# Hybrid encoder layer in fp32r, 1 core: warm-up matmuls on a constant, the second input piece cast in two parts, the second raw input in one transfer

## The chip, the core and the metric

The kernel runs on one core of a Trainium2 chip. The metric is the device time of one execution in microseconds (us). Names of engines: PE is TensorE's matmul, PEld its weight load, DVE is VectorE, ACT is ScalarE, POOL is GpSimd, SP is SyncE, which here only issues transfers (DMA). Times of the timeline count from the start of the profiled span.

## The reference

One layer on a sequence of 1024 frames with 1024 features, all in float32:

```
h = x @ w_in + b_in                     # 1024 x 6144, split in xa za xb zb ga gb
ya = rg_lru(causal_conv4(xa)) * silu(za)          # a scan over the frames
yb = multiscale_pool(xb) * silu(zb)               # windows 2, 4, 8, 16
y  = (sigmoid(ga) * (ya @ w_proj_a) + sigmoid(gb) * (yb @ w_proj_b)) @ w_out + b_out
out = layer_norm(2**0.25 * x + y) * ln_gain + ln_bias
```

The five large products are x @ w_in (1024 x 1024 x 6144), the two projections and w_out (each 1024 x 1024 x 1024), and the pooling product of four 256 x 256 blocks.

## The kernel before, in words

**Products.** Every float32 operand is split into two fp32r parts: `hi` is a cast on ScalarE, `lo` is the raw value minus `hi`, on VectorE (`split`, L450). A product then is three matmuls: hi x hi, hi x lo, lo x hi (`passes`, L454). In a row of the profile `ps_s<-x13l,w0h` is such a matmul: output tile, moving operand, stationary operand. The large products use a seven-product scheme on 2 x 2 blocks, so that sums of input quarters are operands too: `t13` (`t` in the rows) is such a sum of raw input (`sum57`, L1042).

**Order of the work.** Nothing is emitted directly. Each instruction is recorded as a task (`Plan`, L162; the line that emits all of them later is L388, which therefore stands in nearly every row of the profile). `Plan.order` (L252) then plays the tasks through with an estimated duration for each (`cost`, L214) and a due time that is counted back from the matmul that needs the result. TensorE and GpSimd keep the order in which the program recorded their work; ScalarE, VectorE and SyncE take, of what is ready, the task that is due first. So a change of a few tasks can change the order of others on these three engines, wherever due times or free buffers shift.

**Transfers.** Transfers of SP and ACT share eight completion semaphores in turn. The ninth transfer is issued only when the first has landed, and so on.

**The start.** The input arrives transposed in four pieces q of 128 x 2048, each as two raw tiles of 128 x 1024: `xr[q][0]` and `xr[q][1]`. Their halves of 512 columns are four quarters (kh, h) of the piece (`raws`): the first half of `xr[q][0]` is (0,0), its second half is (1,1), the first half of `xr[q][1]` is (0,1), called `xb`, and the second is (1,0), called `x`. Quarters (0,0) and (1,1) are the tiles `x13h` and `x13l`. The first product takes two blocks of weights, `w0r` raw, `w0h` and `w0l` split, and runs quarter by quarter as data comes in (`mm0`), each quarter with both blocks, in four output banks `ps_s`. For piece 0 the quarter (0,0) is loaded, cast, subtracted and multiplied in two parts of 256 columns (`PARTS`), all other quarters in one of 512.

Before it, six matmuls of 128 x 512 zeros run into a bank that nobody reads (`WARM`, L954 to L958). Their operand `warm` is the first half of a work tile of the pool `kt`, which VectorE sets to zero.

**The rest.** 22 groups for the branches a, g (gates) and b follow to about 496 us, then the projections and the output product to 731 us, and a last layer norm with its stores to 738.3 us. The change has no code there.

Of the kernel before, what the change touches and what calls it, by code (L numbers as in the profile page):

```python
# [11 lines left out]
F32 = mybir.dt.float32  # L12
F32R = mybir.dt.float32r
AF = mybir.ActivationFunctionType
ALU = mybir.AluOpType

P = 128
# [3 lines left out]
H = 512  # L21
# [2 lines left out]
EPS = 1e-5  # L24
WINDOWS = (2, 4, 8, 16)
PAD = 16
WARM = 6
NW = 10
NR = 4
NWORK = 10  # L30
# [370 lines left out]
def layer_kernel(ctx: ExitStack, tc: tile.TileContext, xq, x, w_in, par, wg, w_pool, wpa, wpb, w_out, rows, out):  # L401
# [16 lines left out]
    def xt(name, dt=F32R, shape=(P, 2, H)):  # L418
        return xpool.tile(list(shape), dt, tag="x", name=name)
# [7 lines left out]
    def kt(name, dt=F32):  # L427
        return kpool.tile([P, S], dt, tag="k", name=name)
# [4 lines left out]
    def bank(name):  # L433
        return psum.tile([P, H], F32, tag="ps", name=name)
# [5 lines left out]
    HALF = [slice(0, H), slice(H, S)]  # L440
    V, A = nc.vector, nc.scalar
# [508 lines left out]


    begin = ctx.enter_context(ExitStack())
    pass
    warm = kt("warm", F32R)[:, :H]  # L954
    V.memset(warm.bitcast(F32), 0.0)
    psw = bank("ps_warm")
    for i in range(WARM):
        nc.tensor.matmul(psw, warm[:, 0:P], warm, start=True, stop=True)  # L958
# [4 lines left out]
    xr = [[kt(f"xr{q}_{i}", F32) for i in range(2)] for q in range(KQ)]  # L963
# [7 lines left out]
    def dma_w0(n, a, b, h=slice(0, 2)):  # L971

        (A if a == 0 else nc.sync).dma_start(w0_part(wr, n, a, b)[:, h], w_in[first[n]].rearrange("p (h k) m -> p h k m", h=2)[:, h, a:b, :])

    def split_w0(n, a, b, h=slice(0, 2)):
        split(*(w0_part(t, n, a, b)[:, h] for t in (wr, wh, wl)))

    def dma_x(q, i, sl=slice(0, S)):
        nc.sync.dma_start(xr[q][i][:, sl], xq[q, i][:, sl])
# [10 lines left out]
    def split_x(q, kh, h, sl=slice(0, H)):  # L990
        i, p = raws[kh, h]
        split(xr[q][i][:, HALF[p]][:, sl], *(t[:, sl] for t in quarter(q, kh, h)))
# [3 lines left out]
    def mm0(q, kh, h, n, cs=slice(0, H)):  # L996
        sl = slice(q * P, (q + 1) * P)
        passes(ps0[n][h][:, cs], (wh[n][:, kh, sl], wl[n][:, kh, sl]), tuple(t[:, cs] for t in quarter(q, kh, h)),
               q == 0 and kh == h and cs.start == 0, q == KQ - 1 and kh != h)


    PARTS = [slice(0, H // 2), slice(H // 2, H)]
# [4 lines left out]
    dma_w0(0, 0, 1, slice(1, 2))  # L1007
    dma_w0(1, 0, 1)
    dma_x(0, 0, HALF[1])
    dma_x(0, 1, HALF[0])  # L1010
    dma_x(0, 1, HALF[1])
    dma_w0(0, 1, 2)
    dma_x(1, 0)
    dma_w0(1, 1, 2)
# [10 lines left out]
    t13, t24 = [None] * KQ, [None] * KQ  # L1025
# [15 lines left out]

    def sum57(q):  # L1042
        t13[q] = xt(f"t13_{q}", F32)
        r = xr[q][0].rearrange("p (i s) -> p i s", i=2)
        V.tensor_tensor(t13[q], r, xr[q][1][:, HALF[0]].unsqueeze(1).to_broadcast((P, 2, H)), ALU.subtract)

# [35 lines left out]
    for kh, h in ((0, 0), (1, 1), (0, 1), (1, 0)):  # L1082
        if kh == h == 1:
            split_w0(0, 0, 1, slice(1, 2))
        for sl in PARTS if kh == h == 0 else (slice(0, H),):
            split_x(0, kh, h, sl)
            mm0(0, kh, h, 0, sl)
        if kh == h == 1:
            split_w0(1, 0, 1)
            mm0(0, 0, 0, 1)  # L1090
        if kh or h:
            mm0(0, kh, h, 1)
# [6 lines left out]
    w = weights_steps(1)  # L1099
    lower, upper = (0, 1), (2, 3)  # L1100
    each(sum57, lower)
    parts(2)
    each(hi57, lower)
    each(lo57, lower)
    parts(3)
    hi(w.ra, w.pair("wa", (1, 2))[0])
    each(sum57, upper)
    lo(w.ra, *w.tiles["wa"])
    w.sums75(wt("sb_A0", F32))
# [247 lines left out]
    for i, (n, j) in enumerate(steps):  # L1357
# [10 lines left out]
        for g in range(KQ):  # L1368
# [5 lines left out]
            for q in range(KQ):  # L1374
                sl = slice(q * P, (q + 1) * P)
# [10 lines left out]
            if (n, j) in DONE:  # L1386
                d, h = DONE[n, j]
# [198 lines left out]
```

## Time and profile before

| | |
|---|---|
| times of three runs | 740.8, 741.32, 739.7 us; median 740.8 |
| the profiled execution | 740.07 us, of which the span is 738.3 |
| granted TensorE clock, mean | 0.998 |
| busy: PE / DVE / ACT / POOL | 99% / 81% / 62% / 9% of the span |
| bytes moved by DMA | 158.98 MB, mean 215 GB/s |

The profile is that of one execution. The time of an execution is a little longer than its span, here by 1.8 us, which lies around the first and last instruction. A row of the timeline has the start, the time the instructions of the row took, the engine, the operation, output and inputs with their shapes, how many instructions stand in the row, and in brackets for how long the engine had been idle and on whom it waited. Matmuls overlap: the time of one is longer than the distance to the next.

### The profile page before, as it was taken

What the parts mean: (1) busy time and instruction counts of PE and PEld (TensorE: products, weight loads), DVE (VectorE), ACT (ScalarE), POOL (GpSimd) and SP (SyncE); (2) the same over time, 40 slices, a digit from 0 to 9 for tenths busy, and PEclk for the clock granted to TensorE, in tenths of its full rate; (3) what the DMA queues carried; (4) which work ended last, traced back from release to release, by engine and by line L of the source; (5) the groups of instructions that cost most, each with busy time, mean ns of one, the idle gap of its engine ahead of it and who ended that gap; (6) DMA issues with size and microseconds to landing.
All of it is one profiled execution on the core that took longest, in us unless ns stands there. A gap on an engine that the chain in (4) does not pass through costs nothing.

```text
span 738.3 us, 8785 instructions
## 1 busy us (share of the span) xinstructions
PE 729.5 (99%) x3249; PEld 599.4 (81%) x3249; DVE 600.8 (81%) x741; ACT 459.0 (62%) x587; POOL 67.9 (9%) x119
## 2 busy tenths in 40 slices
PE   9999999999999999999999999999999999999996
PEld 7887888888787878788888888888888888888885
DVE  7999796969696878977986768879948786999686
ACT  7686959686877868688844445447553545315473
POOL 0171011111101111100011100100000000000021
PEclk9999999999999999999999999999999999999999
DMA  9247979588988989842187954999679996758748
GB/s 320 111 142 198 264 180 279 135 240 224 303 161 217 328 206 282 219 113 91 54 204 154 212 114 158 278 315 331 235 241 303 311 333 234 267 201 232 196 80 149
DMA packets 64227, 158.98 MB, mean 215 GB/s; under 512 B 4340, under 2 KB 8308, under 8 KB 64120
## 3 DMA queue, kind: packets, MB, share of 16 engines
q1 hardware_dynamic: 43512, 106.26, 41.4%
q0 software_dynamic: 20112, 51.91, 33.6%
q8 instruction: 25, 0.41, 0.2%
q10 hardware_dynamic: 560, 0.26, 0.1%
q14 instruction: 18, 0.15, 0.1%
HBM read 137.43 MB, written 77.07 MB: 291 GB/s over the span
## 4 chain that ended last, share of the span: by engine, by line
PE 99%; DVE 1%; DVEq 0%; issue 0%
PE a_A L388 11%; PE a_B L388 11%; PE a_G L388 11%; PE oa L388 6%; PE pa_a L388 6%; PE pa_b L388 6%; PE c_B L388 6%; PE c_A L388 6%; PE c_G L388 5%; PE ps_s L388 3%; PE oc L388 3%; PE pc_b L388 3%; PE pc_a L388 3%; PE ps_pool L388 3%; PE e_B L388 3%; PE e_A L388 3%
## 5 line engine op out<-in xcount | busy, mean ns | idle before, releaser
L388 ACT ACT_TABLE_LOAD x38 | 48.8, 1283 | 3.0 <-issue 2.3
L388 DVE TENSOR_TENSOR i<-i,xc 128x1024 f32<-128x1024 f32 x8 | 9.8, 1225 | 26.9 <-ACT i L388 26.9
L388 DVE SCALAR_TENSOR_TENSOR xc<-xp,par_sb,xc 128x1023 f32<-128x1023 f32 (+2 forms) x24 | 30.7, 1281 | 0.5
L388 PE MATMUL pa_a<-oh,oh 128*128 128x512 f32 x64 | 24.9, 389 | 0.0
L388 PE MATMUL pa_a<-ol,oh 128*128 128x512 f32 x64 | 24.9, 389 | 0.0
L388 PE MATMUL pa_a<-oh,ol 128*128 128x512 f32 x64 | 24.9, 389 | 0.0
L388 PE MATMUL pa_b<-oh,oh 128*128 128x512 f32 x64 | 24.9, 389 | 0.0
L388 PE MATMUL pa_b<-ol,oh 128*128 128x512 f32 x64 | 24.9, 389 | 0.0
L388 PE MATMUL pa_b<-oh,ol 128*128 128x512 f32 x64 | 24.9, 389 | 0.0
L388 ACT ACTIVATE zb<-zb,par_sb 128x1024 f32<-128x1024 f32 (+1 forms) x16 | 15.0, 938 | 14.2 <-DVE zb L388 14.1
L388 ACT ACTIVATE r<-ps_g,par_sb 64x512 f32<-64x512 f32 x32 | 21.9, 683 | 2.1 <-DVE rb_B L388 0.8
L388 ACT ACTIVATE i<-ps_g,par_sb 64x512 f32<-64x512 f32 x32 | 21.9, 684 | 1.9 <-DVE r L388 1.4
L388 PE MATMUL c_A<-x64h,wd_A 128*128 128x512 f32 x64 | 21.0, 389 | 0.0
L388 PE MATMUL c_B<-x64h,wd_B 128*128 128x512 f32 x64 | 21.0, 389 | 0.0
L388 POOL DMA_DIRECT2D out<-y x7 | 8.5, 1210 | 130.0 <-ACT sd L388 117.4
L388 PE MATMUL ps_pool<-mixh,wp 128*128 128x512 f32 x64 | 20.3, 389 | 0.0
L388 PE MATMUL e_A<-x,wah_A 128*128 128x512 f32 x64 | 19.7, 389 | 0.0
L388 PE MATMUL e_B<-x,wah_B 128*128 128x512 f32 x64 | 19.7, 389 | 0.0
L388 POOL COPY paced<-pace 128x1 f32<-128x1 f32 x17 | 6.4, 376 | 130.9 <-ACT pace L388 130.9
L388 PE MATMUL c_G<-x64h,wd_G 128*128 128x512 f32 x56 | 18.4, 389 | 0.0
L388 DVE TENSOR_TENSOR_SCAN r<-a,i 128x1024 f32<-128x1024 f32 x8 | 18.3, 2284 | 0.1
L388 PE MATMUL e_G<-x,wah_G 128*128 128x512 f32 x56 | 17.2, 389 | 0.0
(521 smaller groups left out, 2534.5 us busy)
## 6 DMA issues: line engine op xcount, KB each, us to landing
sg<-sg SPq DMA_DIRECT2D x16, 512.0 KB, 4.3
ra_A<-in_w_in SPq DMA_DIRECT2D x8, 512.0 KB, 7.1
rb_A<-in_w_in SPq DMA_DIRECT2D x8, 512.0 KB, 7.5
xb<-bias SPq DMA_DIRECT2D x4, 1024.0 KB, 12.8
ya<-r SPq DMA_DIRECT2D x8, 512.0 KB, 5.7
xb<-in_x POOLq DMA_DIRECT2D x4, 1024.0 KB, 8.8
ra_B<-in_w_in SPq DMA_DIRECT2D x8, 512.0 KB, 4.3
rb_B<-in_w_in SPq DMA_DIRECT2D x8, 512.0 KB, 6.6
```

The costliest lines, as they stand in the source:

```text
L388: getattr(getattr(nc, t.op[0]), t.op[1])(*a, **k)
```

## The change

It has four parts.

1. The warm-up matmuls read the constant zero of 128 x 1 that the program's own preamble sets, repeated along the free dimension, in place of the work tile; VectorE's memset falls away, and so does the work tile. There are eight instead of six.
2. The quarter (1,1) of piece 0 is cast, subtracted and multiplied in two parts of 256 columns, like (0,0). (`kh else` is true for kh = 1; for (0,0) the parts were there already, by the same expression: `PARTS if kh == h else`.)
3. The sum `t13` of piece 0 is done by two instructions of 512 columns instead of one of 1024.
4. `xr[0][1]` comes in one transfer of 128 x 1024 instead of two of 128 x 512.

```diff
-WARM = 6
+WARM = 8
...
-    warm = kt("warm", F32R)[:, :H]
-    V.memset(warm.bitcast(F32), 0.0)
+    warm = tc.nc.const_aps.tensor(0.0, [P, H]).bitcast(F32R)
     psw = bank("ps_warm")
     for i in range(WARM):
         nc.tensor.matmul(psw, warm[:, 0:P], warm, start=True, stop=True)
...
     dma_x(0, 0, HALF[1])
-    dma_x(0, 1, HALF[0])
-    dma_x(0, 1, HALF[1])
+    dma_x(0, 1)
     dma_w0(0, 1, 2)
     dma_x(1, 0)
...
     def sum57(q):
         t13[q] = xt(f"t13_{q}", F32)
+        if q == 0:
+            for i in range(2):
+                V.tensor_tensor(t13[q][:, i, :], xr[q][0][:, HALF[i]], xr[q][1][:, HALF[0]], ALU.subtract)
+            return
...
     for kh, h in ((0, 0), (1, 1), (0, 1), (1, 0)):
         if kh == h == 1:
             split_w0(0, 0, 1, slice(1, 2))
-        for sl in PARTS if kh == h == 0 else (slice(0, H),):
+        for sl in PARTS if kh == h else (slice(0, H),):
             split_x(0, kh, h, sl)
             mm0(0, kh, h, 0, sl)
```

The rows below are the order of instructions on an engine, before and after; a number behind a name is that of the buffer, which the change shifts.

TensorE at the start, before. `ps_s_0` and `ps_s_1` are the output banks; the first six real matmuls are the quarter (0,0), then comes (1,1):

```order
L388 MATMUL ps_warm<-warm 128x512 x6
L388 MATMUL ps_s_0_150<-x13h_142,w0h_145 128x256
L388 MATMUL ps_s_0_150<-x13l_147,w0h_145 128x256
L388 MATMUL ps_s_0_150<-x13h_142,w0l_152 128x256
...
L388 MATMUL ps_s_1_168<-x13h_142,w0h_145 128x512
L388 MATMUL ps_s_1_168<-x13l_147,w0h_145 128x512
L388 MATMUL ps_s_1_168<-x13h_142,w0l_152 128x512
L388 MATMUL ps_s_0_178<-x13h_142,w0h_165 128x512
```

and with the change:

```order
L388 MATMUL ps_warm<-const-float32-0.0 128x512 x8
L388 MATMUL ps_s_0_149<-x13h_141,w0h_144 128x256
...
L388 MATMUL ps_s_1_164<-x13h_141,w0h_144 128x256
L388 MATMUL ps_s_1_164<-x13l_146,w0h_144 128x256
L388 MATMUL ps_s_1_164<-x13h_141,w0l_151 128x256
L388 MATMUL ps_s_1_164<-x13h_141,w0h_144 128x256
L388 MATMUL ps_s_1_164<-x13l_146,w0h_144 128x256
L388 MATMUL ps_s_1_164<-x13h_141,w0l_151 128x256
L388 MATMUL ps_s_0_178<-x13h_141,w0h_166 128x512
```

Three matmuls of 512 columns have become six of 256; from `ps_s_0_178` on the order is that of before, to the end of the program.

VectorE behind the quarter (0,0), before (`w0l_172` is the second block of weights):

```order
L388 TENSOR_TENSOR x13l_147<-xr_0_89,x13h_142 128x512
L388 TENSOR_TENSOR w0l_172<-w0r_106,w0h_165 128x2x128
L388 TENSOR_TENSOR t_0_175<-xr_0_89,xr_1_95 128x1024
L388 TENSOR_TENSOR xb_170<-xr_1_95,xb_170 128x512
L388 TENSOR_TENSOR x_0_180<-xr_1_95,x_0_180 128x512
L388 TENSOR_TENSOR x13l_201<-xr_0_99,x13h_195 128x512
```

and with the change:

```order
L388 TENSOR_TENSOR w0l_173<-w0r_102,w0h_166 128x2x128
L388 TENSOR_TENSOR t_0_183<-xr_0_89,xr_1_95 128x512
L388 TENSOR_TENSOR xb_181<-xr_1_95,xb_181 128x512
L388 TENSOR_TENSOR x_0_189<-xr_1_95,x_0_189 128x512
L388 TENSOR_TENSOR t_0_183<-xr_0_89,xr_1_95 128x512
L388 TENSOR_TENSOR x13l_207<-xr_0_98,x13h_201 128x512
```

The first half of the sum still stands ahead of `xb`, the second half now behind `x`.

SyncE's transfers with what they wait for, before (`DMAHW0` and the others are the completion semaphores):

```order
L388 DMA xr_0_89<-in_xq 128x512
L388 DMA xr_1_95<-in_xq 128x512 x2
L388 DMA xr_0_99<-in_xq 128x1024 [waits DMAHW0_49]
L388 DMA w0r_87<-in_w_in 128x2x128 [waits DMAHW1_49]
L388 DMA w0r_106<-in_w_in 128x2x128 [waits DMAHW2_49]
L388 DMA xr_1_108<-in_xq 128x1024 [waits DMAHW3_49]
```

and with the change:

```order
L388 DMA xr_0_89<-in_xq 128x512
L388 DMA xr_1_95<-in_xq 128x1024
L388 DMA xr_0_98<-in_xq 128x1024
L388 DMA w0r_87<-in_w_in 128x2x128 [waits DMAHW0_49]
L388 DMA w0r_102<-in_w_in 128x2x128 [waits DMAHW1_49]
L388 DMA xr_1_107<-in_xq 128x1024 [waits DMAHW2_49]
```

With one transfer less, the first transfer of piece 1 (`xr_0_98`) is the eighth and waits for none; each later one waits for the landing of an earlier transfer than before.

Besides, the planner moves some rows later in the program: on ScalarE the cast of the last columns of the second weight block comes ahead of the cast of the sum of piece 1; on SyncE a few loads of weights and stores of intermediate results change places with a neighbour (the first near 42 to 50 us); on VectorE some sums and subtracts of weights do (near 56 and 426 us, and in the merge of the branches).

More of the change, by code (lines that the diff above doesn't have):

```diff
@@ L952, in layer_kernel @@
     begin = ctx.enter_context(ExitStack())
-    pass
-    warm = kt("warm", F32R)[:, :H]
-    V.memset(warm.bitcast(F32), 0.0)
+    warm = tc.nc.const_aps.tensor(0.0, [P, H]).bitcast(F32R)
     psw = bank("ps_warm")
```

## The prediction, written before the changed kernel had run

> **What bounds the kernel now.** I read the page's shares and chain first, then the busy time by stage, then the first 10 us instruction by instruction, since all of the change lies there.
>
> ```profile
> span 738.3 us, 8785 instructions
> PE 729.5 (99%) x3249; PEld 599.4 (81%) x3249; DVE 600.8 (81%) x741; ACT 459.0 (62%) x587; POOL 67.9 (9%) x119
> PE 99%; DVE 1%; DVEq 0%; issue 0%
> ```
>
> TensorE is busy for 99% of the span and carries 99% of the chain. The windows (stretch, its length, then busy time of PE, PEld, DVE, ACT, POOL; last PEclk, DMA share, GB/s) show where it is not:
>
> ```profile
> 1.44:4.38 2.94, 2.93 (x6) 1.82 (x6) 0.21 (x1) 1.94 (x4) 0.00 (x0) 1.00 0.87 244
> 4.38:9.00 4.62, 4.62 (x16) 3.72 (x17) 4.26 (x9) 3.20 (x7) 0.00 (x0) 1.00 1.00 318
> 20.00:731.00 711.00, 710.94 (x3180) 584.72 (x3179) 581.50 (x710) 445.31 (x563) 67.03 (x98) 1.00 0.75 213
> 731.00:738.30 7.30, 0.00 (x0) 0.00 (x0) 4.00 (x8) 0.29 (x1) 0.00 (x0) 0.75 0.68 144
> ```
>
> From 20 us on TensorE has no gap (710.94 of 711), and what follows 731 is the last layer norm and store, which the change leaves alone. So only what TensorE gains or loses before its gapless part begins can reach the end.
>
> ```profile
> 0.24 0.10 POOL L1578 MEMSET const-float32-0.0<- 128x1 f32 x1 [0.24 <-issue]
> 0.90 0.48 DVE L388 MEMSET warm<- 128x512 f32 x1 [0.90 <-PEq L1578]
> 1.44 2.93 PE L388 MATMUL ps_warm<-warm 128*128 128x512 f32 x6 [1.44 <-DVE warm L388]
> 4.04 0.29 ACT L388 CAST w0h<-w0r 128x128 fp32r<-128x128 f32 x1
> 4.38 0.58 PE L388 MATMUL ps_s<-x13h,w0h 128*128 128x256 f32 x1
> 4.77 0.46 PE L388 MATMUL ps_s<-x13l,w0h 128*128 128x256 f32 x1
> 5.24 0.41 PE L388 MATMUL ps_s<-x13h,w0h 128*128 128x256 f32 x1
> 5.45 0.41 PE L388 MATMUL ps_s<-x13l,w0h 128*128 128x256 f32 x1
> ```
>
> Read these by the distance between starts, since the durations overlap. The first real matmul starts 0.05 after the cast of w0h ends (4.04 + 0.29 = 4.33); it waits for data, not for the warm-up. At the speed of the start a 256-column matmul takes 0.21 (5.24 to 5.45), but the first one behind the wait takes 0.39: a wait costs some 0.18 more than its own length.
>
> ```profile
> 4.17 0.42 DVE L388 TENSOR_TENSOR x13l<-xr,x13h 128x256 fp32r<-128x256 f32 x1 [2.79 <-ACT x13h L388]
> 4.31 0.40 ACT L388 CAST x13h<-xr 128x256 fp32r<-128x256 f32 x1
> 5.08 0.62 ACT L388 CAST x13h<-xr 128x512 fp32r<-128x512 f32 x1 [0.17 <-DMA xr<-in_xq]
> 5.73 0.69 DVE L388 TENSOR_TENSOR x13l<-xr,x13h 128x512 fp32r<-128x512 f32 x1 [0.36 <-ACT x13h L388]
> 5.88 0.67 PE L388 MATMUL ps_s<-x13h,w0h 128*128 128x512 f32 x1
> 6.47 0.79 PE L388 MATMUL ps_s<-x13l,w0h 128*128 128x512 f32 x1
> 7.07 0.63 PE L388 MATMUL ps_s<-x13h,w0l 128*128 128x512 f32 x1
> 7.49 0.44 PE L388 MATMUL ps_s<-x13h,w0h 128*128 128x512 f32 x1
> 7.77 0.40 PE L388 MATMUL ps_s<-x13l,w0h 128*128 128x512 f32 x1
> 8.01 0.40 PE L388 MATMUL ps_s<-x13h,w0l 128*128 128x512 f32 x1
> ```
>
> ```profile
> PEld ps_s L388 <- DVE x13l L388: 0.4, 1, 0.4
> ```
>
> Here is the one stall that the change can remove, in the timeline and in the list of waits. The matmul on x13l waits until VectorE has subtracted the whole 512 columns (5.73 + 0.69 = 6.42, start 6.47). Distances of starts: 0.59, 0.60, then 0.42, then 0.28, then 0.24. The 512-column step is 0.42 where nothing waits, so the pair at 5.88 and 6.47 loses 0.59 + 0.60 - 2 x 0.42 = 0.35. Behind 7.49 the step halves: full speed comes at about 7.58 (of the 0.28 some 0.1 at the slow rate, the rest at the fast one). PEclk reads 1.00 throughout, so I go by the steps and not by that column.
>
> **The change part by part.** *Second piece in two parts.* ScalarE's first half-cast starts at 5.08 as before and takes 0.40 instead of 0.62: done 5.48. VectorE is then free, and its first 256 columns run about 5.52 to 5.94. TensorE reaches its seventh real matmul at 5.88 as before, now of 256 columns, and its eighth, on an x13l that is ready at 5.99, at 6.17 with the 0.18 behind a wait, instead of 6.09 (0.08 lost). The second parts (ScalarE to 5.88, VectorE to 6.36) are there before the eleventh matmul. So the six 256-column matmuls start at 5.88, 6.17, 6.38, 6.59, 6.81, 7.02, and the matmul that started at 7.49 starts at 7.23: 0.26 earlier. Price of the split: three matmuls, a cast and a subtract more, all inside these times.
>
> What the 0.26 is worth depends on when full speed comes. If that stays at 7.58, TensorE has done 0.26 us more of work at half speed, and later saves 0.13. If full speed moves forward by as much as the work does, it saves all of it.
>
> *The warm-up.* TensorE waits 1.44 for a VectorE memset; the constant is set at 0.24. VectorE could start at 0.90 and two other engines at 0.72:
>
> ```profile
> 0.72 3.55 SPq L388 DMA_DIRECT2D xr<-in_xq  x6
> 0.72 1.55 ACTq L388 DMA_DIRECT2D w0r<-in_w_in  x3
> ```
>
> So I put TensorE's first matmul at 0.85, 0.59 earlier. Six warm-up matmuls ran from 1.44 to about 4.17, that is 0.43 each and 0.17 for the first; eight end at 0.85 + 0.17 + 8 x 0.43 = 4.46. The first real one can start its weights at 4.38 and needs its 0.18 of start-up, to 4.56. Two more warm-up matmuls thus cost nothing, with 0.10 to spare; cover gone, each 0.1 of a later start costs 0.1. The direct gain is zero, since w0h sets the 4.38. What it can change is the moment of full speed. No row shows that rule: bounds are 0 (it stays at 7.58) and 0.59 earlier (it follows the first matmul, 6.14 behind it as now), worth half of that, 0.3. I take the lower end with a little of the upper: one execution shows a fixed moment no better than a following one.
>
> The Trainium skill has a rule for it, page "TensorE: Matmul & The Clock Gate", section "Part 1: The HAM clock gate": a monitor lets all clock pulses through only at the end of a window of about 3.4 us in which the array was busy. By that rule, with windows counted back from 7.58 to 4.17 and 0.76, a first matmul at 0.85 just misses the earliest one: this term is 0 and the sum 0.13, unless the windows of an execution lie 0.1 later. The trace agrees in that the step halves once and at once; it can't show where a window begins.
>
> *Merged transfer, first sum in halves.*
>
> ```profile
> 6.00:6.75 0.75, 0.75 (x3) 0.31 (x3) 0.75 (x3) 0.41 (x2) 0.00 (x0) 1.00 0.86 311
> 4.32 1.31 SPq L388 DMA_DIRECT2D w0r<-in_w_in  x2
> 6.34 0.62 ACT L388 CAST xb<-xr 128x512 fp32r<-128x512 f32 x1 [0.34 <-DMA xr<-in_xq]
> 6.67 1.22 DVE L388 TENSOR_TENSOR t<-xr,xr 128x1024 f32<-128x1024 f32 x1
> 7.04 0.62 ACT L388 CAST x<-xr 128x512 fp32r<-128x512 f32 x1
> 7.81 0.69 DVE L388 TENSOR_TENSOR xb<-xr,xb 128x512 fp32r<-128x512 f32 x1
> 8.49 0.62 ACT L388 CAST x13h<-xr 128x512 fp32r<-128x512 f32 x1 [0.84 <-DMA xr<-in_xq]
> 8.93 0.62 PE L388 MATMUL ps_s<-xb,w0h 128*128 128x512 f32 x2
> ```
>
> ScalarE starts on the two halves at 6.34 and 7.04, as they land. One transfer lands whole, so the first half comes when the second did: about 7.0. Then the cast of xb runs to 7.65, half the sum (half of 1.22) to about 7.62, and the subtract of xb (0.69) from 7.70 to 8.39. Its first reader is the second xb matmul, 0.23 behind 8.93, at 9.16, or 9.03 once TensorE is 0.13 ahead. So 0.6 is left: cost nothing. The second half of the sum lies behind the subtract of x and costs about 0.07 of VectorE, which then has to wait for input anyway (next fence). One semaphore lane falls free, so the next input's transfer is issued without waiting for an earlier landing; the DMA engines were 86% busy at 311 GB/s in 6.00:6.75, so a gap of at most 0.14 x 0.75 = 0.1 us there is what it can win.
>
> *What caps a gain.*
>
> ```profile
> 11.67 1.23 DVE L388 TENSOR_TENSOR t<-xr,xr 128x1024 f32<-128x1024 f32 x1 [0.56 <-DMA xr<-in_xq]
> 16.29 1.29 DVE L388 TENSOR_TENSOR w0l<-w0r,w0h 128x512 fp32r<-128x512 f32 x2
> 17.55 0.39 PE L388 MATMUL ps_s<-x13h,w0l 128*128 128x512 f32 x1
> ```
>
> VectorE waits for a transfer until 11.67 and then works without a break to the w0l that TensorE reads at 17.55. The first of the two ends half of 1.29 behind 16.29, at 16.94: 0.61 ahead of its reader, less 0.05 of handing over and 0.18 for a matmul that had to wait. So at most about 0.4 of gain passes 17.55, or 0.6 if that transfer lands 0.2 sooner.
>
> *Later in the program* the planner's order of TensorE is the same; some loads and VectorE rows change places far from their readers. I cost that at nothing: cover is the gapless row above, in which a stall would show at once.
>
> **The sum.** Split 0.13 (bounds 0.13 to 0.26), moment of full speed 0.1 (0 to 0.3), transfer and sum 0 (0 to 0.1 gained); together 0.25 gained of the profiled execution's 740.07: 739.8. That execution is one of four times shown (740.8, 741.32, 739.7 and it), whose mean is 740.47; the median of the three is 740.8. I forecast against the mean: 740.47 - 0.25 = **740.2 us**.
>
> **The rivals.**
>
> *Full speed comes earlier* (0.25). Counted from the first matmul it comes at 6.99; the matmul of 7.49 then starts at about 7.1 and the gain is about 0.4, at the cap: 740.1. Or it can come only at moments a fixed time apart, and an earlier busy start reaches the moment before: then everything to 9 us runs at the pace of its data and the gain is the cap again, 0.4 to 0.6: 739.9 to 740.1. For it: the step halves only once, 3.2 us behind the first real matmul and 6.14 behind the first of all, so that the earlier start may count. Against: 2.9 us of warm-up without a pause have not brought it at 4.4. (By the rule of the Trainium skill on the page named above, that is an execution in which a window begins just behind the first matmul.)
>
> *The merged transfer stalls TensorE* (0.12, slower). xb's subtract is ready 1.4 behind the landing, so it decides from a landing at 7.03 + 0.6 = 7.6. If the merged transfer shares the engines with the next input, now issued beside it, it could land as late as that did (8.47, just ahead of the cast at 8.49): ready 9.9 against 9.03, 0.87 late plus 0.18 for the wait, less the 0.13 gained: 0.92 slower, 741.4. Against: its packets are queued first.
>
> *TensorE doesn't start earlier* (0.10; the change doesn't do what it says). If something else than the memset held it to 1.44, eight warm-up matmuls end at 5.05, the first real one comes half a us late, and the removed stall just pays for it: about 0.1 either way, 740.5.
>
> **How the numbers follow.** My forecast has 0.50, the three above 0.47; 0.03 stays for what I don't see. Runs of the kernel before spread over 1.6 us, six times the gain, so the range comes from that spread: a median of a few runs lies within about 1.0 of its mean, **739.2 to 741.2**. A measurement can tell 0.2% (1.5 us) from no change. No case reaches that; only chance of the runs and the remainder do: faster 0.07, no change 0.89, slower 0.04.
>
> **What would show it.** Right: the first warm-up matmul at 0.8 to 0.9, the first real one still at 4.38, no 0.4 wait on x13l, six 256-column steps of 0.21, the first x13h matmul of w0h's second half at about 7.23, and TensorE 0.1 to 0.4 ahead at 17.55 and at 731. Full speed at 7.0 instead of 7.58 speaks for the first rival; TensorE waiting for xb near 9 for the second; a first matmul at 1.4 for the third. Wrong altogether: a gap of TensorE behind 20 us, from a swapped load or VectorE row, or a landing of the first pieces that the order of transfers has moved.

## The result: slower by 0.23%

The changed kernel takes 742.13 us (median of 22 runs, 739.9 to 744.85), the kernel before 740.71 (22 runs, 739.66 to 742.62). The ratio is 1.0023, with a 95% interval of 1.0015 to 1.0032. That lies above the predicted range of 739.2 to 741.2.

The 22 runs fall into two groups, which the mean granted clock tells apart: 11 at 0.997 or 0.998 took 739.9 to 741.75 (median 741.03), 11 at 0.992 to 0.995 took 742.52 to 744.85 (median 743.76). The median of all, 742.13, lies between the two groups. So one half lost 0.3 us against 740.71 and the other half some 3. Both need an explanation, and the first profile shows an execution of the better half. Its page:

```profile
span 739.3 us, 8792 instructions
PE 729.5 (99%) x3254; PEld 599.3 (81%) x3254; DVE 600.5 (81%) x742; ACT 459.8 (62%) x588; POOL 68.1 (9%) x119
```

The windows of the same execution (stretch, length, busy time of PE, PEld, DVE, ACT, POOL, then PEclk, DMA share, GB/s):

```profile
6.00:6.75 0.75, 0.75 (x5) 0.64 (x5) 0.27 (x1) 0.00 (x0) 0.00 (x0) 1.00 0.76 270
6.75:7.50 0.75, 0.10 (x1) 0.00 (x0) 0.00 (x0) 0.00 (x0) 0.00 (x0) 1.00 1.03 409
7.50:8.25 0.75, 0.00 (x0) 0.00 (x0) 0.00 (x1) 0.44 (x2) 0.00 (x0) 1.00 1.02 365
...
20.00:731.00 711.00, 711.00 (x3179) 584.82 (x3179) 582.45 (x711) 446.15 (x563) 66.35 (x98) 1.00 0.75 213
```

From 20 us to 731 TensorE is as gapless as before. The new thing stands at 6.75 to 8.25: TensorE and VectorE stand still, and ScalarE until 7.8, while the DMA engines are fully busy. The list of TensorE's waits has one entry for it, which the profile of the kernel before didn't have, and the start in rows shows it:

```profile
PE ps_s L388 <- ACT w0h L388: 1.4, 1, 1.4
PE ps_warm L388 <- PEq L1579: 0.8, 1, 0.8
```

```profile
0.77 3.54 PE L388 MATMUL ps_warm<-const-float32-0.0 128*128 128x512 f32 x8 [0.77 <-PEq L1579]
...
4.40 0.38 PE L388 MATMUL ps_s<-x13h,w0h 128*128 128x256 f32 x1
...
5.50 0.76 DVE L388 TENSOR_TENSOR x13l<-xr,x13h 128x256 fp32r<-128x256 f32 x2
...
5.57 0.34 PE L388 MATMUL ps_s<-x13h,w0h 128*128 128x256 f32 x1
5.99 0.39 PE L388 MATMUL ps_s<-x13l,w0h 128*128 128x256 f32 x1
...
6.56 0.28 PE L388 MATMUL ps_s<-x13h,w0l 128*128 128x256 f32 x1
7.81 0.41 ACT L388 CAST w0h<-w0r 128x256 fp32r<-128x256 f32 x1 [2.03 <-DMA w0r<-in_w_in]
8.12 0.62 ACT L388 CAST xb<-xr 128x512 fp32r<-128x512 f32 x1
8.27 0.50 PE L388 MATMUL ps_s<-x13h,w0h 128*128 128x512 f32 x1 [1.42 <-ACT w0h L388]
8.60 0.40 PE L388 MATMUL ps_s<-x13l,w0h 128*128 128x512 f32 x1
```

The warm-up starts at 0.77, the first real matmul at 4.40 as before, full speed is there from 3.95 on (by the trace's record of the granted clock), and the second piece is done at 6.84 (6.56 + 0.28). Then the matmul that had started at 7.49 waits until 8.27 for the cast of `w0h`, and that cast, at 7.81, waits for the transfer of the second block of raw weights. I call this transfer w0r(1): 128 rows of 2 x 128 columns, ScalarE's third. In the profile of before it had landed at 5.45, and its cast stood at 5.60 without a wait, between two others; here it lands at 7.79. The row of before:

```profile
5.60 0.40 ACT L388 CAST w0h<-w0r 128x256 fp32r<-128x256 f32 x1
```

### The profile page after: what moved, and what is told of

The parts are those of the page before. It is cut to its first block, busy times and chain, and to the rows that moved or that the text cites. A ratio compares the mean times of both kernels' runs of the same rounds, so it can differ in the third digit from the quotient of the medians.

```text
span 739.3 us, 8792 instructions
## 1 busy us (share of the span) xinstructions
PE 729.5 (99%) x3254; PEld 599.3 (81%) x3254; DVE 600.5 (81%) x742; ACT 459.8 (62%) x588; POOL 68.1 (9%) x119
## 4 chain that ended last, share of the span: by engine, by line
PE 98%; DMA 1%; DVE 0%; ACTq 0%; DVEq 0%; ACT 0%; issue 0%
PE a_A L388 11%; PE a_B L388 11%; PE a_G L388 11%; PE oa L388 6%; PE pa_b L388 6%; PE pa_a L388 6%; PE c_B L388 6%; PE c_A L388 6%; PE c_G L388 5%; PE oc L388 3%; PE pc_b L388 3%; PE pc_a L388 3%; PE ps_pool L388 3%; PE e_B L388 3%; PE e_A L388 3%; PE ps_s L388 3%
```

## The experiments

**First: which part does it.** Two theories on the transfers, both with part 4 at fault: the freed lane lets the next input run beside w0r(1); or the merged transfer's rows, of 4 KB instead of 2 KB, hold up the 512-byte rows of w0r(1). On the half of the runs with the lower clock: the gap of TensorE brings it, or the new warm-up does. Four runs.

*Part 4 undone:*

```diff
-    dma_x(0, 1)
+    dma_x(0, 1, HALF[0])
+    dma_x(0, 1, HALF[1])
```

> The change with its fourth part undone: xr[0][1] comes in two transfers again, so the first transfer of piece 1 waits for a landing as before; warm-up, parts of the second piece and halves of the sum stay. All theories (freed lane, or larger packets) put the fault into part 4: the second weight block w0r(1) lands at about 5.45 again instead of 7.79, TensorE has no gap of 1.4 us near 6.8, full speed still comes near 3.9, the first matmul on the second block starts near 6.7, and the time is 0.4 to 0.6 below that of the kernel before (740.1 to 740.3), with granted clocks of 0.997 or more in every run. If the warm-up or the split were to blame, the time would stay near 742 and the gap too.

Measured 742.46 us, 1.0025 times before (1.0016 to 1.0034): not what any of the theories said, though the start was nearly as expected. w0r(1) landed at 6.85 and the gap was 0.4. Two of the nine runs had a mean clock of 0.995, where 0.997 or more had been expected. Its waits of TensorE:

```profile
PE c_G L388 <- ACT wbh_G L388: 0.9, 1, 0.9
...
PE c_G L388 <- DVE wbl_G L388: 0.6, 1, 0.6
PE ps_s L388 <- ACT w0h L388: 0.4, 1, 0.4
```

`c_G` is a product near 51 us, far from the edit. The planner, played through with one more transfer, had put three subtracts of `x64l` and one of `wd_G` ahead of the sums that `wbh_G` needs. So undoing a part of the change had also changed the order of other work, and the run tells little on part 4.

*Part 4 alone, on the kernel before:*

```diff
-    dma_x(0, 1, HALF[0])
-    dma_x(0, 1, HALF[1])
+    dma_x(0, 1)
```

> The kernel before with the fourth part alone: xr[0][1] in one transfer, nothing else. Both transfer theories: w0r(1) lands at 7.5 to 7.9 instead of 5.45, TensorE waits for the cast of it from about 7.5 to 8.3, 0.5 to 0.9 us slower than before (741.2 to 741.6). If part 4 does harm only together with the earlier warm-up: no change, 740.7.

742.93 us, 1.0025 (1.0014 to 1.0035). w0r(1) landed at 8.64 and TensorE waited 1.9:

```profile
PE ps_s L388 <- ACT w0h L388: 1.9, 1, 1.9
```

Part 4 does harm without the others; the size was above what I expected, since the clock fell too (below), in six of the eleven runs.

*Merged transfer, but the next input waits again* (a transfer of 8 KB ahead of it makes it the ninth):

```diff
     dma_x(0, 1)
+    with nc.within(0):
+        nc.sync.dma_start(par_sb[0:16, :], par[0:16, :])
     dma_w0(0, 1, 2)
...
-    nc.sync.dma_start(par_sb, par)
+    nc.sync.dma_start(par_sb[16:P, :], par[16:P, :])
```

> The change, with 16 rows of the parameters (8 KB) loaded as a transfer of their own behind the merged one, so that the first transfer of piece 1 is the ninth again and waits for the first landing; the merged transfer stays. Freed-lane theory (piece 1 beside w0r(1) is what delays it): w0r(1) lands near 5.5 again, merged transfer near 7.0, no gap near 7, 740.2 to 740.5. Larger-packet theory (rows of 4 KB instead of 2 KB take the share of w0r(1)'s 512-byte rows): w0r(1) still lands past 7, the gap stays, 741 to 743.

742.08 us, 1.0016 (1.0007 to 1.0026); w0r(1) landed at 8.49. The freed lane is not the cause: with the lane's wait back, the landing is as late. The rows of 4 KB stay in question.

*The gap filled with matmuls on the constant:*

```diff
         if kh == h == 1:
             split_w0(1, 0, 1)
+            for i in range(7):
+                nc.tensor.matmul(psw, warm[:, 0:P], warm, start=True, stop=True)
             mm0(0, 0, 0, 1)
```

> The change, with seven more matmuls on the constant put where TensorE has its gap, ahead of the first matmul on the second weight block; nothing else. It tests the spread of the change's runs (739.9 to 744.9, about half of them near 743.7 at a mean granted clock of 0.992 to 0.995). Gap theory (the gap is what lets the clock fall back, or not rise, in some executions): no run above 742, granted clock 0.997 or more in all, time about 741.0. If the earlier or constant-fed warm-up is the cause of those runs: about half of them stay near 743.7.

All seven runs had a mean clock of 0.997 or 0.998, against 11 of 22 without the filler. So the gap is what brings the lower clock, not the warm-up; the run of part 4 alone, which has the lower clock too, still has the old warm-up. The time was 743.02 (1.0025, 1.0015 to 1.0036), from 741.76 to 743.86, so "no run above 742" was wrong. The one profile is of the run of 741.76: w0r(1) landed at 7.56 there, and the fillers kept TensorE busy to 8.24. A landing near 9.05, as two profiles of the change have it below, would leave a gap of 1.3 us behind the fillers, which is an estimate for the slower runs and not seen.

**Second: the parts on a fixed order.** From here on every edit is made behind the planner, on its list of the kernel before, so that all that follows the start is in the old order on every engine:

```diff
     def emit(self):
         order = self.order()
...
-            for t in order:
+            for op, args, kw in self.edited(order):
```

`edited` drops, splits or replaces the tasks of the start by a list `DO` of the parts of the change: 1 the warm-up (the work tile is still set aside), 2 the second piece in parts, 3 the sum in halves, 4 the merged transfer. Its core, for 1, 2 and 4:

```diff
+            if 1 in DO and name == "ps_warm":
+                warm += 1
+                for _ in range(1 + (WARM2 - 6 if warm == 6 else 0)):
+                    yield t.op, (out, zero[:, 0:P], zero), t.kw
+                continue
+            if 2 in DO and name in ("x13h0", "x13l0") and out.offset() >= H:
+                for sl in (slice(0, H // 2), slice(H // 2, H)):
+                    yield t.op, tuple(a[:, sl] if isinstance(a, Ref) else a for a in t.args), t.kw
+                continue
...
+            if 4 in DO and t.op[1] == "dma_start" and name == "xr0_1":
+                if out.offset() == 0:
+                    yield t.op, self.whole, t.kw
+                continue
```

*Parts 1 to 3:*

```diff
+DO = (1, 2, 3)
```

> Warm-up, second piece in parts, sum in halves; two transfers; and every later instruction in the order of the kernel before (the edit is made behind the planner). The run of the change with the two transfers back lost 0.9 + 0.6 us at two matmuls on wbh_G and wbl_G near 51 us, where VectorE and ScalarE had another order. Theory that this order is an accident of the planner: no wait near 51 us here, 1.5 us less than that run's 742.46, so 740.4 to 741.0, between no change and 0.4 faster than before. Theory that the earlier start itself runs into late data there: the wait is here too, 742 again. w0r(1) lands between 5.4 and 6.9.

740.16 us against 740.8 of before, measured beside it, 0.9992 (0.9983 to 1.0000), and all eleven runs between 739.76 and 740.38. No wait near 51 us: the 2.3 us between this and the first experiment were the planner's order, 1.5 of them the two waits on `c_G` above. The range of 740.4 to 741.0 was too careful. w0r(1) was late here too, but by less (a row of ScalarE's timeline and one of TensorE's, as in the fences of this kind below):

```profile
7.21 0.41 ACT L441 CAST w0h<-w0r 128x256 fp32r<-128x256 f32 x1 [1.43 <-DMA w0r<-in_w_in]
...
7.67 0.50 PE L441 MATMUL ps_s<-x13h,w0h 128*128 128x512 f32 x1 [0.72 <-ACT w0h L441]
```

*All four parts:*

```diff
+DO = (1, 2, 3, 4)
```

> All four parts on the order of the kernel before. If the loss of the change lies in the start alone (w0r(1) landing past 7.5, a gap of TensorE of 1.4 to 2.3 us, and a fall of the clock for 3.4 us where a window of the gate holds the whole gap): as the change, median 741 to 743.5, about half of the runs at a mean clock under 0.996, and 1 to 2 us slower than the same kernel with two transfers. If the planner's later order makes the loss: 740.2 to 740.8.

742.56 us, 1.0027 (1.0017 to 1.0038), six of twelve runs at 0.993 to 0.995. So the changed kernel's loss is there with the old order, and part 4 costs 2.4 us against the three others, measured side by side on one chip. In its profile, of a run without the fall of the clock, w0r(1) landed at 7.70:

```profile
PE ps_s L441 <- ACT w0h L441: 1.4, 1, 1.4
```

The planner's later swaps, which I had costed at nothing, made no difference that these runs show in the changed kernel (1.0023 with them).

*Two transfers again, but of 64 rows of 4 KB* (parts 1 to 3 otherwise):

```diff
+            if 6 in DO and t.op[1] == "dma_start" and name == "xr0_1":
+                rows = slice(0, 64) if out.offset() == 0 else slice(64, P)
+                yield t.op, tuple(x[rows, :] for x in self.whole), t.kw
+                continue
```

> As the one with parts 1 to 3 on the old order, but xr[0][1] comes in two transfers of 64 rows x 1024 (4 KB a row) instead of two of 128 rows x 512 (2 KB a row): number of transfers, bytes and waits are the same. Row-size theory (a queue's turn is one row, so longer rows beside it slow w0r(1) with its 512-byte rows): w0r(1) lands past 7, TensorE has a gap, 741.5 to 743. If it is the single transfer or its completion that hurts: w0r(1) lands at 5.4 to 6.9 and the time is that of the kernel with 2 KB rows.

741.15 us, 1.0007 (0.9998 to 1.0016): 1.0 more than with rows of 2 KB, where transfers, bytes and waits are the same.

```profile
8.23 0.40 ACT L441 CAST w0h<-w0r 128x256 fp32r<-128x256 f32 x1 [2.32 <-DMA w0r<-in_w_in]
...
8.69 0.50 PE L441 MATMUL ps_s<-x13h,w0h 128*128 128x512 f32 x1 [1.71 <-ACT w0h L441]
```

With rows of 4 KB w0r(1) lands at 8.21, though nothing was merged. That doesn't bring all of the loss: 1.0 of 2.4 us, since none of the eleven runs had a mean clock below 0.996. It is not quite a test of the row size alone: by the trace's packet records most of these rows took 0.27 us, against 0.16 for a row of 4 KB in the merged transfer.

*w0r(1) moved to SyncE's queue*, behind the second half of `xr[0][0]` and ahead of `xr[0][1]` (parts 1 to 3, two transfers of 2 KB rows):

```diff
+            if 5 in DO and t.op[1] == "dma_start" and name == "xr0_1" and out.offset() == 0:
+                w = next(u for u in order if u.op[1] == "dma_start" and u.args[0].tile.name == "w0r1" and u.eng == "ACT")
+                yield ("sync", "dma_start"), w.args, w.kw
+            if 5 in DO and t.op[1] == "dma_start" and name == "w0r1" and t.eng == "ACT":
+                continue
```

> Parts 1 to 3 on the old order, with the transfer of w0r(1) moved from ScalarE's queue to SyncE's, between the second half of xr[0][0] and xr[0][1]. If w0r(1) is late because it shares the engines turn by turn with SyncE's queue, it now lands before xr[0][1] in every execution, at 5.3 to 5.9, and xb some 0.3 later than before; no gap near 7, no run with a mean clock under 0.996, and full speed from 4 to 7.4: 0.3 to 0.7 faster than before, 740.0 to 740.5. If w0r(1)'s landing is not what TensorE waits for, the time is that of the kernel without this edit.

739.88 us, 0.9988 (0.9979 to 0.9996), the fastest version of all, 0.9 below before and a little below what was expected. No run's clock was below 0.996, and w0r(1) was there in time:

```profile
6.02 0.41 ACT L441 CAST w0h<-w0r 128x256 fp32r<-128x256 f32 x1 [0.26 <-DMA w0r<-in_w_in]
...
6.75 0.40 PE L441 MATMUL ps_s<-x13h,w0h 128*128 128x512 f32 x1
...
8.13 0.86 PE L441 MATMUL ps_s<-xb,w0h 128*128 128x512 f32 x2
```

TensorE goes from the second piece to the second block without a gap; what is late next is `xb` (0.86 for the pair at 8.13 where 0.62 is usual).

**Third: single parts, and the test of the cause.** Part 1 alone, then part 2 alone, on the old order:

```diff
+DO = (1,)
```

> Part 1 alone (eight warm-up matmuls on the constant, no memset) on the order of the kernel before. If the earlier full speed is what the two-transfer version gains by: 740.2 to 740.5, nearly all of its 0.6. If it needs the split of the second piece too: 740.6 to 740.9.

Part 1 alone: 740.65 us, 0.9999 (0.9991 to 1.0008).

```diff
+DO = (2,)
```

> Part 2 alone (second piece cast, subtracted and multiplied in two parts of 256) on the order of the kernel before, old warm-up. By the term of the prediction: 0.13 faster, 740.6 to 740.7. If TensorE then waits for w0h of the late w0r(1) instead: no change at all, 740.8.

Part 2 alone: 740.59 us, 0.9998 (0.9989 to 1.0007). Neither gives anything by itself that these runs can show; the 0.13 us of my sum would be a ratio of 0.9998, which they can't tell from 1. Full speed came at about 4.0 in the profile of part 1 alone, but TensorE then waits for its data; the waits of the two kernels, one after the other:

```profile
...
PE ps_s L441 <- DVE xb L441: 0.3, 1, 0.3
PE ps_s L441 <- DVE x13l L441: 0.2, 1, 0.2
PE ps_s L441 <- ACT w0h L441: 0.2, 1, 0.2
```

```profile
...
PE ps_s L441 <- ACT w0h L441: 0.5, 1, 0.5
PE ps_s L441 <- DVE xb L441: 0.3, 1, 0.3
```

With part 2 alone the wait on x13l is gone from TensorE's list, and a wait of 0.5 on w0h stands in it.

*All four parts, w0r(1) on SyncE's queue ahead of the merged transfer:*

```diff
+DO = (1, 2, 3, 4, 5)
```

> All four parts on the old order, with the transfer of w0r(1) moved to SyncE's queue ahead of the merged transfer, as in the fastest version so far (739.88, which had two transfers). If part 4 hurts only through w0r(1) beside it: w0r(1) lands at 5.9 to 6.1, no gap on w0h, no run with a mean clock under 0.996; xb comes some 0.7 later, so TensorE waits up to 0.6 us for it near 8.3: 740.0 to 740.7, two us below the version with w0r(1) on ScalarE's queue. If the merged transfer or the unheld transfer of piece 1 hurts by itself: 741 or more.

740.13 us, 0.9994 (0.9985 to 1.0003), no run's clock below 0.997: 2.4 us less than the four parts with w0r(1) on ScalarE's queue. The merged transfer and the freed lane are still there, and TensorE now waits 0.2 us for `xb`. So part 4 hurts through w0r(1) beside it, and through nothing else of that size. The clock says the same: with the merged transfer beside w0r(1) and no filler, 27 of 57 runs had a mean of 0.995 or less, with w0r(1) ahead of it none of 11, and with rows of 2 KB beside it 3 of 42.

```profile
6.14 0.41 ACT L441 CAST w0h<-w0r 128x256 fp32r<-128x256 f32 x1 [0.34 <-DMA w0r<-in_w_in]
...
6.77 0.40 PE L441 MATMUL ps_s<-x13h,w0h 128*128 128x512 f32 x1
...
8.84 0.50 PE L441 MATMUL ps_s<-xb,w0h 128*128 128x512 f32 x1 [0.23 <-DVE xb L441]
```

**Fourth: more profiles of the two kernels.** What was open: how the clock falls in the changed kernel itself, and whether 5.45 is usual for before.

> The kernel before once more, unchanged, for a second profile of it. In the first profile w0r(1) landed at 5.45; in the two kernels with the same transfers it landed at 6.86 and 7.19. If the landing varies from execution to execution: past 6 here, TensorE waits for w0h before its matmul of 7.49, which starts at 7.6 or later, and the time is above 740.07. If the early landing belongs to the kernel before: 5.4 to 5.6 again. Full speed comes at another moment than 7.58 if the windows of the clock gate have no fixed place in the execution.

740.01 us; w0r(1) at 5.71, full speed at 6.17 (the trace's record of the granted clock begins with the first step to full speed; its start is the moment I give here and below).

> A third profile of the kernel before. w0r(1) landed at 5.45 and 5.71 in its two profiles, and at 6.86 to 7.19 in four kernels with the same first transfers. If that is chance of the execution: as likely 6.9 to 7.2 here, with a time of 740.5 or more. If it belongs to this kernel: under 6 again, with a time near 740.0.

741.04 us; w0r(1) at 7.30, full speed at 6.18:

```profile
7.33 0.40 ACT L388 CAST w0h<-w0r 128x256 fp32r<-128x256 f32 x1 [1.56 <-DMA w0r<-in_w_in]
...
7.78 0.50 PE L388 MATMUL ps_s<-x13h,w0h 128*128 128x512 f32 x1 [0.50 <-ACT w0h L388]
```

So the landing is chance of the execution, and the kernel before already waits for w0h in some of them. The three executions with the times 740.07, 740.01 and 741.04 go with landings of 5.45, 5.71 and 7.30.

> The changed kernel again, unchanged, for another profile. By the explanation so far (w0r(1) late, a gap of TensorE; where a 3.4 us window of the clock gate holds the whole of a gap of about 2 us, the next window runs at half speed): in about half of such looks matmuls of 512 columns start 0.42 apart again for 3.4 us behind the gap, the time is above 742.5, and the gap is 1.9 us or more; in the others 0.23 apart throughout, time 740 to 742. A time above 742.5 without such a stretch, or with a gap of less than 1.5 us, would speak against it.

> A third look at the changed kernel; expected as for the look before it.

> A fourth look at the changed kernel; expected as for the two before it.

The three profiles are of runs of 740.94, 744.97 and 743.83 us, with w0r(1) at 7.07, 9.03 and 9.06. The windows of the second and of the third, cut where PEclk changes:

```profile
5.08:8.49 3.41, 1.72 (x11) 1.31 (x10) 1.09 (x4) 0.71 (x2) 0.00 (x0) 1.00 0.97 334
8.49:11.90 3.41, 2.39 (x6) 1.93 (x7) 2.41 (x5) 2.85 (x7) 0.00 (x0) 0.50 1.00 339
11.90:15.31 3.41, 3.41 (x10) 2.67 (x9) 3.41 (x7) 3.41 (x6) 0.00 (x0) 0.50 0.99 345
15.32:18.70 3.38, 3.38 (x16) 2.77 (x15) 3.38 (x5) 3.38 (x6) 0.00 (x0) 1.00 1.03 416
```

```profile
3.97:7.38 3.41, 2.71 (x14) 1.79 (x12) 1.98 (x6) 1.70 (x6) 0.00 (x0) 1.00 0.93 307
7.38:10.79 3.41, 1.25 (x5) 0.98 (x6) 1.27 (x3) 1.71 (x4) 0.00 (x0) 1.00 1.01 311
10.80:14.20 3.40, 3.40 (x9) 2.63 (x8) 3.40 (x8) 3.40 (x8) 0.00 (x0) 0.50 1.04 384
14.21:17.60 3.39, 3.39 (x16) 2.82 (x15) 3.39 (x5) 3.39 (x6) 0.00 (x0) 1.00 1.03 404
```

Behind the gap the clock stands at 0.50 for two stretches of 3.41 us in the one and for one in the other. In both the matmul behind the gap starts at 9.5 (9.51 and 9.54), so the difference of their spans, 743.2 and 742.0, is the clock alone: (6.83 - 1.02) / 2 = 2.9 us lost to half speed in the one, of whose 6.83 us 1.02 were still gap, and 3.41 / 2 = 1.7 in the other; 2.9 - 1.7 is the 1.2 between them. What is left over the 738.3 of before, 2.0 in both (743.2 - 2.9 and 742.0 - 1.7, less 738.3), is the gap less what the earlier start had gained.

All landings of w0r(1), one profile each:

| beside w0r(1) in SyncE's queue | landings, us |
|---|---|
| rows of 2 KB (before, three profiles) | 5.45, 5.71, 7.30 |
| rows of 2 KB (part 1; part 2; parts 1 to 3 on either order) | 7.05, 6.88, 6.85, 7.19 |
| rows of 4 KB (the change, four profiles) | 7.79, 7.07, 9.03, 9.06 |
| rows of 4 KB (part 4 alone; next input waits; filler; four parts; two transfers of 64 rows) | 8.64, 8.49, 7.56, 7.70, 8.21 |
| w0r(1) itself in SyncE's queue, ahead (two transfers; one) | 6.00, 6.12 |

The trace has the moment at which each of a transfer's sixteen shares is complete. For w0r(1), the first and the last four, in us:

```
before, first profile    4.73 ... 5.30 5.31 5.38 5.45
before, third profile    5.04 ... 6.03 6.12 6.22 7.30
change, first profile    4.96 ... 5.88 7.45 7.56 7.79
change, third profile    4.92 ... 6.87 8.94 8.96 9.03
```

Most of it is there by 6 in every case. Where it is late, one to four shares are: here by 1.1 us (7.30 behind 6.22) with rows of 2 KB, by 1.6 and 2.1 with rows of 4 KB.

The trace also records when each row of a transfer begins to move. In two profiles with a single late share, the rows of w0r(1) that start behind 5.9 and 6.3 are those of that share (in us):

```
change, second profile   5.92 6.09 6.27 6.45 then 6.48 6.50 6.53 6.55 6.58
before, third profile    6.32 6.42 6.53 6.63 6.74 then 6.76 6.78 6.81 6.83 6.85 6.88 6.90
```

A row of w0r(1) itself takes 0.03. They start 0.18 apart in the one and 0.10 in the other, and 0.02 apart at the end. A row of 4 KB of the other queue takes 0.16 there and one of 2 KB 0.08. So the distances are about the sum of one row of each, as if a late share moved one row per row of the other queue, until it has the way to itself. An estimate from these steps: a share has 16 rows (256 of 512 bytes in all), and a turn at each of them would take 2.9 us beside rows of 4 KB and 1.6 beside rows of 2 KB.

## Why the prediction was wrong

**Right.** TensorE carries the time, and only the start matters: 711.00 of 711 us busy behind 20. The warm-up starts early (0.77; I said 0.85) and eight matmuls delay nothing (first real one at 4.40). Full speed does come earlier, at 3.95, 4.47, 5.08 and 3.97 in the four profiles of the change, against 7.58, 6.17 and 6.18 before: what I gave to a rival. Part of that is chance of the execution, since the nine other kernels with the new warm-up have it at 3.94 to 6.21 and two with the old one at 5.19 and 6.48; the steps at 0.76, 4.17 and 7.58 from which I put the gain at nothing were those of one execution. The wait on x13l shrinks, from 0.44 us in the rows of the weight loads to 0.28, but doesn't go: in the first profile the matmul on x13l still starts 0.42 behind the one before it (5.57 to 5.99). The sum in halves and the later swaps show no cost. Together parts 1 to 3 gain 0.64 us (by the interval between none and 1.3), somewhat more than the 0.25 of my sum, whose terms as written add to 0.23, and the 0.4 of its cap.

**The step that failed** is "Merged transfer, first sum in halves", with its "cost nothing". I asked who reads the merged transfer (`xb`, with 0.6 us to spare) and gave the next input's free lane 0.1 us to win. I did not ask which transfer is in flight beside it in another queue and who waits for that one. It was w0r(1), issued by ScalarE at 1.66, just ahead of the merged one at 2.11, and its reader was the next matmul of the part that I had just made earlier: in my own walk, TensorE comes for w0h at 7.23, and I had no row for when w0h is ready. The landing of 5.45 in the one profile made it look harmless. What the runs showed in place of "nothing": w0r(1) landing at 7.07 to 9.06, a wait of 0.7 to 2.7 us for w0h, and 2.4 us for part 4 over the three other parts. My last sign of being wrong, a landing that the order of transfers has moved, named this kind of thing, but without a wait or a price.

**The slower rival** was near and still wrong: it let the merged transfer itself land late, at `xb`, decided from 7.6 us on, and priced 0.92. The transfer did land at 7.85, 8.41, 8.09 and 8.15 in the four profiles, past my point, but no wait on `xb` is longer than 0.2 us there. TensorE itself came later by the wait for w0h, so part of that stall may be hidden behind it; with w0r(1) out of the way and a landing at 7.41 the wait on `xb` is 0.2. And its cause, the next input beside it, fell with the run in which that input waits.

**The term that wasn't there at all** is the fall of the clock: 1.7 and 2.9 us in the two profiles that have it, the larger part of the 2.9 and 4.0 by which their runs exceed the one of 740.94, which does not have it and whose gap is 0.7. I treated full speed as something that comes once.

**One execution as the basis.** The split's 0.13 was worked out for an execution in which w0h is ready at 6.0. With w0r(1) landing near 7, as in five of seven profiles with rows of 2 KB, TensorE next waits for w0h, 0.5 us in the profile of part 2 alone, and such a wait can take the whole gain. Whether it did is not shown: the 0.9998 of that run fits 0.13 as well as nothing. I had asked what is late next for `xb` and for the w0l read at 17.55, and not for w0h.

**What stays open.** Why a few of the sixteen shares still have rows to move when the other queue's rows come, in some executions and not in others of the same kernel; and why 64-row transfers of 4 KB rows, with w0r(1) at 8.21 in their one profile, had no run with a fallen clock in eleven. In that profile the gap of 1.7 us lies across two stretches of the clock, of which neither is emptied by half (below); of the ten other runs no trace shows the gap.

## What to carry to other kernels

When a transfer is made larger or issued earlier, look beyond its own readers: list what is in flight in the other queues at that time, with small rows above all, and find the instruction that waits for it. Put a transfer that the bounding engine needs soon into the same queue ahead of the large one, which here was worth 2.4 us with the same bytes. And test a part of a change on a fixed order: where a planner orders the work, undoing one line moved other work and cost some 2 us by itself.

## What the runs showed of the hardware

The clock of TensorE moved in steps of 3.41 us from some start that differs by execution, as the cut windows above show. What raised it and let it fall can be read from the busy time of the stretch ahead of each step. The stretches ahead of full speed, of the kernel before and then of the change (first profiles):

```profile
0.76:4.16 3.40, 2.72 (x6) 1.82 (x6) 0.48 (x1) 1.72 (x3) 0.60 (x17) 1.00 0.65 190
4.17:7.57 3.40, 3.38 (x11) 2.56 (x11) 3.04 (x7) 2.82 (x7) 0.00 (x0) 1.00 0.99 340
```

```profile
0.54:3.94 3.40, 3.17 (x8) 2.52 (x8) 0.00 (x0) 1.48 (x2) 0.65 (x17) 1.00 0.57 161
...
7.37:10.77 3.40, 2.50 (x11) 1.87 (x12) 2.52 (x5) 2.96 (x7) 0.00 (x0) 1.00 0.97 354
```

TensorE busy for 80% of a stretch (2.72 of 3.40) did not raise the clock, 93% (3.17) did: that is what the earlier warm-up bought where a stretch began near 0.54. Once up, it stayed behind a stretch of 74% (2.50, with the gap's end in it), and in the run with 64-row transfers behind one of 61% (2.07; the gap's other end left the stretch before it at 83%). It fell behind 50% (1.72) and 37% (1.25), and in the run of part 4 alone behind 44%. So here, as an estimate, the fall needed somewhere between 1.3 us (39% of 3.41) and 1.7 us of idle time in one and the same stretch. The first two rows are of part 4 alone, the third of the 64-row transfers:

```profile
6.48:9.88 3.40, 1.49 (x6) 0.89 (x6) 0.69 (x2) 1.22 (x3) 0.00 (x0) 1.00 1.04 366
9.89:13.30 3.41, 3.41 (x9) 2.64 (x8) 3.41 (x6) 3.26 (x8) 0.00 (x0) 0.50 1.04 387
...
7.36:10.76 3.40, 2.07 (x9) 1.53 (x10) 2.09 (x4) 2.53 (x6) 0.00 (x0) 1.00 1.05 359
```

The Trainium skill, page "TensorE: Matmul & The Clock Gate", section "Part 1: The HAM clock gate", has windows of 3413 ns that run on their own; the trace agrees, with 3.41. It lets the clock fall after an idle window of some 3.4 us; here gaps of 1.9 us (part 4 alone) to 2.7 were enough, with work on both sides of them.

The other surprise is how late the rest of a small transfer can be: of the 128 KB of w0r(1) most is there by 6 us, and the last shares come up to 3 us behind. The Trainium skill, page "DMA: Bandwidth & Descriptors", section "Queues, rings and completion order", has each DMA engine take turns between queues, a packet at a time. The row starts above agree with such turns, here of one row each: 0.18 us beside rows of 4 KB and 0.10 beside rows of 2 KB.
